# Strassen's seven block products in the up projection of a one-core decoder layer

## The chip, the cores and the metric

The kernel runs on one core of a Trainium2 chip. The metric is the device time of one execution in microseconds (us), the median of several. A core has TensorE (PE in the profile; its weight loads are PEld), VectorE (DVE), ScalarE (ACT), GpSimd (POOL) and SyncE (SP), which here issues every DMA. Each works through its own queue of instructions and waits on semaphores for the others.

## The reference

One decoder layer over 2048 tokens (and 16 meta tokens) of width 1024, all in float32. A first part mixes tokens (a state-space mixer, a retention mixer and an output projection) and normalises. What the change is about is the MLP behind it:

```python
h = layer_norm(DEEPNORM_ALPHA * h + mixed, ln1_g[l], ln1_b[l])
ff = jnp.square(jax.nn.relu(h @ w_up[l])) @ w_down[l]     # w_up 1024 x 4096, w_down 4096 x 1024
h = layer_norm(DEEPNORM_ALPHA * h + ff, ln2_g[l], ln2_b[l])
```

## The kernel before

**Blocks and phases.** The tokens are taken in two blocks of 1024 (`NB = 2`, b = 0 and 1). For each block, phase 1 makes the input projection and both mixers, phase 2 the output projection and first norm, and phase 3 the MLP. Phase 3 walks over the 4096 hidden units in eight groups (g) of four pages of 128 units (`G = 4`, f). A group has an up part (each page times 512 tokens at a time, twice) and a down part (eight tiles of 128 tokens, two halves of 512 output columns each, accumulated on VectorE into `acc`).

**Three products for one.** Every float32 operand is held as a rounded high part and a low part (value minus high part) in the type fp32r, and each product is made as high x high + high x low + low x high. So `mm3` (L265) issues three matmuls for each pair of 128 x 128 weights and 512 moving columns. A group is 8 x 8 x 3 = 192 matmuls up and 16 x 4 x 3 = 192 down.

**Weight pages.** `feed_init` (L123) lists all pages in the order in which they are used. `feed_raw` (L145) has SP load the raw 512-KB page into one of two buffers (`wraw`), as far as one page ahead; a load waits until the last reader of its buffer is done. `feed_one` (L154) splits a page: ScalarE copies the high part (L169), VectorE subtracts it for the low part (L171). At most eight pages live at once; `free` gives one back. `get` makes a page at once if it isn't there.

**Order.** The program order of each engine is the order in which the Python code emits instructions (`manual_schedule`). What is put between the matmuls is set by `tick` (L65): it runs callbacks that are due, one step of a background generator (`pump`), and one `feed`. In phase 3 there is a tick at half and at the end of every 24-matmul product of the up part (`marks=(3, 7)`), and one in each 12-matmul tile of the down part (`marks=(3,)`), ahead of that tile's addition. `rest_norm` (L469) is such a generator: in block 0 it normalises the eight token tiles of block 1, one in nine steps.

**Results of the up part.** A product sits in one of four PSUM banks of the pool `big`. ScalarE takes the relu (L1149) and its square as the high part (L1150), VectorE squares again (L1151) and subtracts (L1152). In the down part VectorE adds each PSUM tile to `acc` (L1179; in group 0 L1176).

Of the kernel before, what the change touches and what calls it, by code (L numbers as in the profile page):

```python
# [17 lines left out]
D = 1024  # L18
SEQ = 2048
NM = 16  # L20
NH = 6
# [11 lines left out]
KORDER = (2, 3, 4, 5, 6, 0, 1, 7)  # L33
ALPHA = 2.0 ** 0.25
# [9 lines left out]
class Builder:  # L44
    def __init__(self, tc, a, ctx):
# [7 lines left out]
        self.pgp = pool(name="pgp", bufs=8)  # L53
        self.ffp = pool(name="ffp", bufs=4)
        self.wrawp = pool(name="wrawp", bufs=2)
        self.bigp = pool(name="bigp", bufs=4, space=PSUM)
# [66 lines left out]
    def feed_init(self):  # L123
        a = self.a
        items = []
        for b in range(NB):
            slab = [[("s", b, h, p), a["wslab"][h, p], "w"] for h in range(NH) for p in range(4)]
            wo = [[("o", b, k), a["w_out"][k * 128:(k + 1) * 128, :], "w"] for k in KORDER]
            wu = [[("wu", b, i), a["wu"][i], "u"] for i in range(2)]
            items += slab[:4] + wu + slab[4:] + wo  # L130
            for g in range(NF // G):
                items += [[("u", b, g * G + f), a["wup"][g * G + f], "w"] for f in range(G)]
                items += [[("d", b, g * G + f), a["w_down"][(g * G + f) * 128:(g * G + f + 1) * 128, :], "w"]
                          for f in range(G)]
        self.items = items
        self.page = {}
        self.live = 0
        self.wu_ok = False
        self.pool_lo = False
        self.feed_every = 1  # L140
        self.ri = 0
        self.si = 0
        self.raws = {}

    def feed_raw(self):  # L145
        while self.ri < len(self.items) and self.ri < self.si + 2:
            key, src, kind = self.items[self.ri]
            if kind != "b":
                t = self.wrawp.tile([128, 1024], F32, tag="wraw", name="wraw")
                self.nc.sync.dma_start(out=t, in_=src)  # L150
                self.raws[self.ri] = t
            self.ri += 1

    def feed_one(self):  # L154
        if self.si >= len(self.items):
            return False
        key, src, kind = self.items[self.si]
        if (self.live >= 8 and kind != "u") or (kind == "u" and not self.wu_ok):
            return False
        self.feed_raw()  # L160
        if kind != "u":
            self.live += 1
        if kind != "b":
            t = self.raws.pop(self.si)
            if kind == "w":
                pg = self.pgp.tile([128, 2, 1024], F32R, tag="pg", name="pg")
            else:
                pg = self.ffp.tile([128, 2, 1024], F32R, tag="ff", name="wu")
            self.nc.scalar.copy(pg[:, 0, :], t)  # L169
            e = self.nc.gpsimd if self.pool_lo else self.nc.vector  # L170
            e.tensor_tensor(out=pg[:, 1, :], in0=t, in1=pg.bitcast(F32)[:, 0, :], op=ALU.subtract)  # L171
        else:
            pg = self.pgp.tile([128, 2, 1024], F32, tag="pg", name="pg")
            self.nc.sync.dma_start(out=pg, in_=src.partition_broadcast(128))
        self.page[key] = pg
        self.si += 1
        self.feed_raw()
# [12 lines left out]
    def free(self, key):  # L190
        del self.page[key]
        if key[0] != "wu":
            self.live -= 1
# [40 lines left out]

    def norm_v(self, t, gb, parts=1, st=None):
# [12 lines left out]
    def to_channels(self, t, hi, lo, tok, n=128):  # L248

        nc = self.nc  # L250
        for kk in range(2):
            ps = self.sm().rearrange("p (k t) -> p k t", k=4)
            for i in range(4):
                k = kk * 4 + i
                nc.tensor.transpose(ps[:, i, :n], t[:n, k * 128:(k + 1) * 128], self.ident[:n, :n])  # L255
# [9 lines left out]
    def mm3(self, ps, pairs, marks=(), pumps=(), first=True, last=True, done=None):  # L265
# [5 lines left out]
        for j, (lh, ll, rh, rl) in enumerate(pairs):  # L271
            for l, r in ((lh, rh), (lh, rl), (ll, rh)):
                nc.tensor.matmul(ps, l, r, start=(i == 0), stop=(i == n - 1))  # L273
# [9 lines left out]
    def build(self):  # L283
        nc, a = self.nc, self.a
        with self.tc.manual_schedule():
# [14 lines left out]
            self.y_d = [[dt(f"y{b}_{k}", [128, TB]) for k in range(8)] for b in range(NB)]  # L300
            self.um_d = dt("um", [NM, S5W])
# [5 lines left out]
            self.tab_d = [dt(f"tab{g}", [128, 2, 256]) for g in range(NG)]  # L307
            for b in range(NB):
                with ExitStack() as s:
                    self.p1 = s.enter_context(self.tc.tile_pool(name=f"p1_{b}", bufs=1))  # L310
                    self.phase1(b)
                    self.phase2_open(b)
                with ExitStack() as s:
                    self.accp = s.enter_context(self.tc.tile_pool(name=f"acc_{b}", bufs=1))
                    self.phase2(b)
                    self.phase3(b)


    def phase1(self, b):
# [29 lines left out]
        for h in range(NH):  # L349
            slab = [self.get(("s", b, h, p)) for p in range(4)]  # L350

            def part(k, i, c0, c1):
                return slab[k // 2][:, i, (k % 2) * 512 + c0:(k % 2) * 512 + c1]
# [115 lines left out]
    def rest_norm(self):  # L469
        nc = self.nc  # L470
        gb = self.gb_rest
        for t in range(NT, NB * NT):
            x = self.accp.tile([128, D], F32, tag="tmp", name="xr", bufs=2)
            nc.sync.dma_start(out=x, in_=self.a["x"][t * 128:(t + 1) * 128, :])
            for _ in range(3):
                yield
            self.norm_v(x, gb)
            for _ in range(4):
                yield
            nc.sync.dma_start(out=self.h_d[t], in_=x)  # L480
            for _ in range(2):
                yield
# [572 lines left out]
    def out_pairs(self, t, hf, k0, k1):  # L1055
        y, c = self.ys[t], slice(hf * 512, hf * 512 + 512)
        wo = lambda k: self.get(("o", self.b, k))
        return [(y[:, 0, k], y[:, 1, k], wo(k)[:, 0, c], wo(k)[:, 1, c]) for k in KORDER[k0:k1]]
# [218 lines left out]
```

## Time and profile before

| what | value |
|---|---|
| time, median of 3 runs | 2498.85 us (2496.75 to 2501.19) |
| the profiled execution | 2497.59 us, span 2495.8 us |
| granted TensorE clock, mean | 0.991 of full speed |
| PE, DVE, ACT, POOL busy in that span | 97%, 51%, 24%, 11% |
| DMA | 200.83 MB, mean 80 GB/s |

The span is the time from the first to the last instruction. Busy shares are means over a program whose phases differ; a busy PE is not PE at its peak, since matmuls are pipelined. Phase 3 takes most of the time: its groups follow each other at about 87 us.

### The profile page before, as it was taken

The numbers are of one execution on the slowest core, as the hardware profiler recorded it, in microseconds if no ns is written. First come the engines' busy times: TensorE is split into PE (matmuls) and PEld (weight loads), VectorE is DVE, ScalarE is ACT, GpSimd is POOL, SyncE is SP. The second block draws the span as 40 slices with busy tenths as digits, with TensorE's granted clock in tenths as the row PEclk, the third lists the DMA queues.
The fourth block names the chain that finished last, engine by engine and source line by source line (L and its number), as shares of the span: only waits on it lengthen the run. The fifth ranks groups of instructions, "written<-read, shape, count | busy, mean of one in ns | idle before, by whom it ended". The sixth has DMA issues, their size and how long they took to land. (4 is left out here: it accounts for less than half of the span.)

```text
span 2495.8 us, 30353 instructions
## 1 busy us (share of the span) xinstructions
PE 2410.0 (97%) x11932; PEld 2066.4 (83%) x11932; DVE 1285.2 (51%) x2770; ACT 602.8 (24%) x1151; POOL 265.2 (11%) x303
## 2 busy tenths in 40 slices
PE   6889999899999999999999999999999999999998
PEld 5778889778888888888889999988888888888886
DVE  6867757656455443334365455656634333333436
ACT  3323322322221122112132222222212212211211
POOL 2322322201000000000031011101000000000004
PEclk9999999999999999999999999999999999999999
DMA  5132253362132221102142422134212111110211
GB/s 198 65 101 86 86 125 101 91 196 68 59 102 86 72 71 60 48 28 68 51 144 90 97 90 78 62 108 158 83 36 68 51 34 51 59 51 26 68 34 68
DMA packets 100767, 200.83 MB, mean 80 GB/s; under 512 B 11360, under 2 KB 52096, under 8 KB 99984
## 3 DMA queue, kind: packets, MB, share of 16 engines
q1 hardware_dynamic: 100624, 198.88, 25.2%
q8 instruction: 94, 1.54, 0.3%
q14 instruction: 49, 0.40, 0.1%
HBM read 160.83 MB, written 39.06 MB: 80 GB/s over the span
## 5 line engine op out<-in xcount | busy, mean ns | idle before, releaser
L273 PE MATMUL big<-act,pg 128*128 128x512 f32 x3648 | 846.5, 391 | 0.0
L273 PEld LDWEIGHTS big<-act,pg 128*128 128x128 f32 x3648 | 681.1, 188 | 142.3 <-issue 2.4
L273 PE MATMUL big<-pg,ff 128*128 128x512 f32 x3072 | 700.8, 389 | 0.0
L273 PEld LDWEIGHTS big<-pg,ff 128*128 128x128 f32 x3072 | 576.1, 188 | 119.3
L273 PE MATMUL big<-pg,act 128*128 128x384 f32 x2304 | 458.7, 349 | 0.8 <-ACT act L256 0.5
L273 PEld LDWEIGHTS big<-pg,act 128*128 128x128 f32 x2304 | 404.3, 192 | 5.3 <-DVE act L257 1.4
L169 ACT CAST pg<-wraw 128x1024 fp32r<-128x1024 f32 x192 | 198.3, 1047 | 624.8 <-PE big L273 549.8
L1179 DVE TENSOR_TENSOR acc<-acc,big 128x512 f32<-128x512 f32 x224 | 153.1, 686 | 357.4 <-PE big L273 357.2
L1151 DVE TENSOR_TENSOR rs<-rs 128x512 f32<-128x512 f32 x128 | 88.5, 691 | 338.3 <-ACT rs L1149 338.2
L171 DVE TENSOR_TENSOR pg<-wraw,pg 128x1024 fp32r<-128x1024 f32 x175 | 211.4, 1222 | 64.7 <-ACT pg L169 58.1
L219 POOL TENSOR_TENSOR ln_rs<-ln_rs,mhalf 128x1 f32<-128x1 f32 (+1 forms) x49 | 61.4, 1253 | 1531.8 <-DVE ln_rs L218 1522.4
L273 PE MATMUL big<-pg,yt 128*128 128x512 f32 x768 | 182.5, 396 | 0.8 <-DVE yt L1008 0.7
L1149 ACT ACTIVATE rs<-big 128x512 f32<-128x512 f32 x128 | 76.6, 598 | 438.1 <-PE big L273 432.5
L273 PEld LDWEIGHTS big<-pg,yt 128*128 128x128 f32 x768 | 144.4, 190 | 32.7 <-DVE yt L1008 2.5
L1152 DVE TENSOR_TENSOR ff<-rs,ff 128x512 fp32r<-128x512 f32 x128 | 88.7, 693 | 14.0 <-DVE rs L1151 0.9
L519 DVE TENSOR_TENSOR t<-big,rope 128x256 f32<-128x256 f32 x96 | 40.5, 422 | 96.6 <-ACT v L512 96.2
L1150 ACT ACTIVATE ff<-rs 128x512 fp32r<-128x512 f32 x128 | 81.0, 633 | 4.1
L534 ACT COPY qkT<-sm 128x256 f32<-128x256 f32 x96 | 35.4, 369 | 156.4 <-PE sm L532 156.2
L550 DVE SCALAR_TENSOR_TENSOR R<-R,sm 128x128 f32<-128x128 f32 x96 | 27.3, 284 | 71.4 <-PE sm L549 71.3
L574 POOL TENSOR_TENSOR gn_sc<-gn_sc,mhalf 128x4 f32<-128x4 f32 x24 | 24.8, 1032 | 345.3 <-DVE gn_sc L572 325.2
L512 ACT ACTIVATE v<-big,cols 128x128 f32<-128x128 f32 x96 | 35.5, 369 | 100.4 <-PE big L273 100.4
L555 ACT COPY o<-sm 128x128 f32<-128x128 f32 x96 | 25.5, 266 | 139.3 <-DVE gn_st L553 134.2
(202 smaller groups left out, 1882.5 us busy)
## 6 DMA issues: line engine op xcount, KB each, us to landing
wraw<-in_wup_dram SPq DMA_DIRECT2D x64, 512.0 KB, 3.7
wraw<-in_w_down_dram SPq DMA_DIRECT2D x64, 512.0 KB, 3.7
wraw<-in_wslab_dram SPq DMA_DIRECT2D x48, 512.0 KB, 3.7
smat<-mat SPq DMA_DIRECT2D x32, 256.0 KB, 3.9
wraw<-in_w_out_dram SPq DMA_DIRECT2D x16, 512.0 KB, 3.8
acc<-h SPq DMA_DIRECT2D x16, 512.0 KB, 3.8
out_dram<-acc SPq DMA_DIRECT2D x14, 512.0 KB, 2.7
y<-yst SPq DMA_DIRECT2D x24, 256.0 KB, 3.3
```

The costliest lines, as they stand in the source:

```text
L169: self.nc.scalar.copy(pg[:, 0, :], t)
L171: e.tensor_tensor(out=pg[:, 1, :], in0=t, in1=pg.bitcast(F32)[:, 0, :], op=ALU.subtract)
L219: nc.gpsimd.tensor_tensor(out=rs[:n, 0:1], in0=rs[:n, 0:1], in1=self.mhalf[:n, 0:1], op=ALU.pow)
L273: nc.tensor.matmul(ps, l, r, start=(i == 0), stop=(i == n - 1))
L512: nc.scalar.activation(out=v2, in_=ps[:, 256:384], func=AF.Copy, scale=self.cols[:, h:h + 1])
L519: nc.vector.tensor_tensor(out=t1, in0=src, in1=c, op=ALU.mult)
L534: nc.scalar.copy(qkT, pt[:, 0:256])
L1149: nc.scalar.activation(out=tmp[:, 0], in_=ps, func=AF.Relu)
L1150: nc.scalar.activation(out=ff[f][:, 0, tk], in_=tmp[:, 0], func=AF.Square)
L1151: nc.vector.tensor_tensor(out=tmp[:, 1], in0=tmp[:, 0], in1=tmp[:, 0], op=ALU.mult)
L1152: nc.vector.tensor_tensor(out=ff[f][:, 1, tk], in0=tmp[:, 1], in1=ff[f].bitcast(F32)[:, 0, tk], op=ALU.subtract)
L1179: nc.vector.tensor_tensor(out=acc, in0=acc, in1=ps, op=ALU.add)
```

## The change

Groups from `CLASSIC[b]` on (2 in block 0, 1 in block 1; 13 of the 16 groups) make their up part with `up_seven`. A pair of pages (q) is seen as a 2 x 2 block matrix (two pages by two halves of the 1024 inputs), and the block of tokens as two halves by two halves. Strassen's algorithm in Winograd's form makes the four result blocks from seven block products in place of eight. A product p is 4 x 3 matmuls for each of the two pairs. Weight sums (`COMBO`) are made on VectorE as each page is fed. Sums of activation blocks are made once for each token block by `left_sums` (for each of four k, eight additions and four splits into high and low part on VectorE, in five steps; eight stores), during the last group of the old kind, and stored in DRAM; one of them is then loaded over a part of `h1T`, the other three are streamed back in every group by `ring_fill`. Results are put together by additions on VectorE from three accumulator banks (A, B, C) for each pair. The background generator `rest_norm` starts a group earlier and takes four steps a tile. Weight pages become units of 512 columns (two to an old page, 16 live), and phase 3 has a pool of 24 pieces of 128 x 512 (`q`, 2 KB in each partition) for hidden activations, sums, the ring and temporaries. The core of the diff:

```diff
+CLASSIC = (2, 1)
+PORDER = (6, 1, 5, 7, 2, 4, 3)
+COMBO = {1: ((None, 0, 0),), 2: ((None, 0, 1),), 3: ((None, 1, 1),),
+         4: ((None, 0, 1), (SUB, 1, 1), (ADD, 1, 0), (SUB, 0, 0)), 5: ((None, 1, 0), (SUB, 0, 0)),
+         6: ((None, 1, 1), (SUB, 1, 0), (ADD, 0, 0)), 7: ((None, 1, 1), (SUB, 1, 0))}
...
+        def pair(key, src1, src2):
+            n = len(self.srcs)
+            self.srcs += [src1, src2]
+            for p in PORDER:
+                self.jobs.append((key + (p,), COMBO[p], (n, n + 1)))
...
     def feed_raw(self):
+        while self.si < len(self.jobs) and self.ri < len(self.srcs) and self.ri < self.jobs[self.si][2][0] + 2:
+            t = self.wrawp.tile([128, 1024], F32, tag="wraw", name="wraw")
+            self.nc.sync.dma_start(out=t, in_=self.srcs[self.ri])
...
     def feed_one(self):
+        need = 0 if kind == "u" else 2 if kind == "w" else 1
+        if self.live + need > 16 or (kind == "u" and not self.wu_ok) or (need == 1 and self.qp is None):
             return False
...
+        elif kind == "w":
+            pg = [self.unit(), self.unit()]
+            for z in range(2):
+                nc.scalar.copy(pg[z][:, 0, :], raw[0][:, z * 512:z * 512 + 512])
+            for z in range(2):
+                e.tensor_tensor(out=pg[z][:, 1, :], in0=raw[0][:, z * 512:z * 512 + 512],
+                                in1=pg[z].bitcast(F32)[:, 0, :], op=ALU.subtract)
         else:
+            pg = self.unit()
+            src = [(op, raw[j][:, z * 512:z * 512 + 512]) for op, j, z in kind]
+            x = src[0][1]
+            if len(src) > 1:
+                t = self.q()
+                for op, y in src[1:]:
+                    nc.vector.tensor_tensor(out=t, in0=x, in1=y, op=op)
+                    x = t
+                self.qfree()
+            nc.scalar.copy(pg[:, 0, :], x)
+            nc.vector.tensor_tensor(out=pg[:, 1, :], in0=x, in1=pg.bitcast(F32)[:, 0, :], op=ALU.subtract)
...
+    def relu2(self, x):
+        nc.vector.scalar_tensor_tensor(out=x, in0=x, scalar=0.0, in1=x, op0=ALU.max, op1=ALU.mult)
+        hi = self.q(F32R)
+        nc.scalar.copy(hi, x)
+        lo = self.q(F32R)
+        nc.vector.tensor_tensor(out=lo, in0=x, in1=hi.bitcast(F32), op=ALU.subtract)
...
+    def left_sums(self, b):
...
+        def split(f, x, k):
+            hi = self.q(F32R)
+            S.copy(hi, f)
+            lo = self.q(F32R)
+            add(lo, f, hi.bitcast(F32), SUB)
+            for i, z in enumerate((hi, lo)):
+                nc.sync.dma_start(out=self.s_d[b][x][:, k, i], in_=z.bitcast(F32))
+            self.qfree(3)
+        for k in range(4):
+            x21, f1 = self.q(), self.q()
+            add(x21, hf[:, k, t2], lf[:, k, t2])
+            add(f1, hf[:, k + 4, t2], lf[:, k + 4, t2])
+            add(f1, f1, x21)
+            yield
...
+    def ring_fill(self, cap):
+        while self.stream and len(self.ring) < cap:
+            x, k = self.stream.popleft()
+            ts = [self.q(F32R) for _ in range(2)]
+            for i in range(2):
+                self.nc.sync.dma_start(out=ts[i].bitcast(F32), in_=self.s_d[self.b][x][:, k, i])
+            self.ring.append(ts)
...
+    def up_seven(self, b, g):
+        for p in PORDER:
+            bank = {1: "A", 2: "A", 6: "B", 7: "B", 4: "B", 5: "C", 3: "C"}[p]
+            first = p in (1, 6, 5)
...
+            w = [self.get(("U", b, g, q, p)) for q in range(NQ)]
+            for k in range(4):
+                if p in left:
+                    k0, tk = left[p]
+                    ah, al = h1[:, k0 + k, tk], l1[:, k0 + k, tk]
+                else:
+                    ah, al = self.ring.popleft()
+                for q in range(NQ):
+                    c = slice(k * 128, k * 128 + 128)
+                    self.mm3(acc[bank, q], [(w[q][:, 0, c], w[q][:, 1, c], ah, al)],
+                             first=first and k == 0, last=k == 3, more=not first)
+                if p not in left:
+                    self.qfree(2)
+                if self.stream:
+                    self.ring_fill(6 if self.stream[0][0] != 2 else 3 if p == 3 else 0)
+                if k == 1:
+                    self.tick()
+            for q in range(NQ):
+                self.free(("U", b, g, q, p))
+                ps, fa, fb = acc[bank, q], 2 * q, 2 * q + 1
+                if p == 6:
+                    s12[q] = self.q()
+                    S.copy(s12[q], ps)
+                elif p == 1:
+                    s21[q] = self.q()
+                    V.tensor_tensor(out=s12[q], in0=s12[q], in1=ps, op=ADD)
+                    S.copy(s21[q], ps)
+                elif p == 5:
+                    s22[q] = self.q()
+                    V.tensor_tensor(out=s22[q], in0=s21[q], in1=ps, op=ADD)
+                elif p == 2:
+                    x = self.q()
+                    S.copy(x, ps)
+                    ff[fa][0] = self.relu2(x)
+                else:
+                    x, f, h = {7: (s22, fb, 1), 4: (s21, fa, 1), 3: (s12, fb, 0)}[p]
+                    V.tensor_tensor(out=x[q], in0=x[q], in1=ps, op=ADD)
+                    ff[f][h] = self.relu2(x.pop(q))
+            self.tick()
...
+            to = list(range(NT)) if g < nc0 else [4, 0, 1, 2, 3, 5, 6, 7] if last else [4, 5, 6, 7, 0, 1, 2, 3]
...
+            if g == nc0 - 1:
+                self.drain_bg()
+                for i in range(2):
+                    nc.sync.dma_start(out=self.h1T[i].bitcast(F32)[:, 0:4, 512:1024], in_=self.s_d[b][1][:, :, i, :])
+                self.qfree(16)
+                self.ring_fill(6)
```

## Rows read from the trace of the kernel before

**Rows 1.** The page, part 1: busy us, share of the span, instructions.
```profile
PE 2410.0 (97%) x11932; PEld 2066.4 (83%) x11932; DVE 1285.2 (51%) x2770; ACT 602.8 (24%) x1151; POOL 265.2 (11%) x303
```

**Rows 2.** The chain that ended last: start us, us, what.
```profile
1637.35 2.09 PE big L273 x12
...
1802.24 677.34 PE big L273 x2988
```

**Rows 3.** Stretch of one group of phase 3: busy us by engine, clock, DMA.
```profile
1976.00:2063.00 87.00, 87.00 (x385) 72.05 (x384) 31.52 (x40) 17.49 (x25) 0.00 (x0) 1.00 0.15 48
```

**Rows 4.** Waits in 1802 to 2480: us in total, times, longest.
```profile
ACT pg L169 <- PE big L273: 274.9, 7, 39.3
...
DVE acc L1179 <- PE big L273: 190.9, 99, 2.0
...
ACT pg L169 <- DMA wraw<-in_w_down_dram: 7.3, 3, 4.8
```

**Rows 5.** Groups by shape: count, busy us, mean ns of one.
```profile
L1179 DVE TENSOR_TENSOR acc<-acc,big 128x512 f32<-128x512 f32 x224 | 153.1, 686 | 357.4 <-PE big L273 357.2
...
L256 ACT CAST act<-sm 128x512 fp32r<-128x512 f32 x64 | 34.3, 589 | 96.1 <-PE sm L255 96.1
```

**Rows 6.** Timeline of VectorE: start us, us, line.
```profile
695.34 0.69 DVE L1176 SCALAR_TENSOR_TENSOR acc<-acc,big 128x512 f32<-128x512 f32 x1 [2.03 <-PE big L273]
695.94 2.35 DVE L171 TENSOR_TENSOR pg<-wraw,pg 128x1024 fp32r<-128x1024 f32 x2
701.41 0.69 DVE L1151 TENSOR_TENSOR rs<-rs 128x512 f32<-128x512 f32 x1 [3.11 <-ACT rs L1149]
702.20 0.69 DVE L1152 TENSOR_TENSOR ff<-rs,ff 128x512 fp32r<-128x512 f32 x1
```

**Rows 7.** Timeline of ScalarE, and of VectorE behind it.
```profile
1995.44 0.60 ACT L1149 ACTIVATE rs<-big 128x512 f32<-128x512 f32 x1 [4.18 <-PE big L273]
1996.07 0.63 ACT L1150 ACTIVATE ff<-rs 128x512 fp32r<-128x512 f32 x1
1996.61 1.03 ACT L169 CAST pg<-wraw 128x1024 fp32r<-128x1024 f32 x1
...
1996.07 0.69 DVE L1151 TENSOR_TENSOR rs<-rs 128x512 f32<-128x512 f32 x1 [3.95 <-ACT rs L1149]
```

**Rows 8.** Timelines of VectorE, SP and ScalarE around one reload of `wraw`.
```profile
2057.52 2.36 DVE L171 TENSOR_TENSOR pg<-wraw,pg 128x1024 fp32r<-128x1024 f32 x2
...
2058.77 6.52 SPq L150 DMA_DIRECT2D wraw<-in_wup_dram  x3
...
2062.63 1.05 ACT L169 CAST pg<-wraw 128x1024 fp32r<-128x1024 f32 x1 [0.65 <-DMA wraw<-in_wup_dram]
```

**Rows 9.** All loads of `wraw` in 1802 to 2480, from issue.
```profile
DMA to landing us min/median/max: 3.4/3.7/5.9
```

**Rows 10.** Stretches around the last matmul, same columns as rows 3.
```profile
2484.00:2486.00 2.00, 1.00 (x5) 0.50 (x3) 1.24 (x2) 1.17 (x1) 2.00 (x1) 1.00 0.00 0
2486.00:2488.00 2.00, 0.00 (x0) 0.00 (x0) 1.97 (x3) 0.00 (x0) 0.77 (x2) 1.00 0.47 193
2488.00:2490.00 2.00, 0.00 (x0) 0.00 (x0) 1.86 (x4) 0.00 (x0) 2.00 (x2) 0.74 0.17 70
2490.00:2492.00 2.00, 0.00 (x0) 0.00 (x0) 2.00 (x4) 0.00 (x0) 0.74 (x1) 0.50 0.63 262
```

**Rows 11.** Timeline of PE near the start.
```profile
21.19 1.97 PE L255 MATMUL sm<-ident,x 128*128 128x128 f32 x8 [4.65 <-DVE x L245]
22.81 5.23 PE L273 MATMUL big<-pg,act 128*128 128x384 f32 x24
```

**Rows 12.** DMA issues: count, KB each, median us to landing.
```profile
gb<-in_ln_gb_dram SPq DMA_DIRECT2D x4, 1024.0 KB, 5.5
```

**Rows 13.** Timeline of VectorE: one tile of `rest_norm`, first and last instruction.
```profile
704.15 1.28 DVE L206 BATCH_NORM_STATS2 ln_st<-xr 128x6 f32<-128x512 f32 x2
...
707.49 1.28 DVE L245 SCALAR_TENSOR_TENSOR xr<-xr,ln_rs,gbrest 128x1024 f32<-128x1024 f32 x1 [0.43 <-POOL ln_rs L219]
```

More of the change, by code (lines that the diff above doesn't have):

```diff
@@ L145, in feed_raw @@
     def feed_raw(self):
[L146 to L151, printed above, removed]
+        while self.si < len(self.jobs) and self.ri < len(self.srcs) and self.ri < self.jobs[self.si][2][0] + 2:
+            t = self.wrawp.tile([128, 1024], F32, tag="wraw", name="wraw")
+            self.nc.sync.dma_start(out=t, in_=self.srcs[self.ri])
+            self.raws[self.ri] = t
@@ L159, in feed_one @@
             return False
         self.feed_raw()
[L161 to L171, printed above, removed]
-        else:
-            pg = self.pgp.tile([128, 2, 1024], F32, tag="pg", name="pg")
-            self.nc.sync.dma_start(out=pg, in_=src.partition_broadcast(128))
+        nc = self.nc
@@ new lines, in feed_one @@
+        raw = [self.raws[i] for i in ids]
+        e = nc.gpsimd if self.pool_lo else nc.vector
+        if kind == "u":
+            pg = self.ffp.tile([128, 2, 1024], F32R, tag="ff", name="wu")
+            nc.scalar.copy(pg[:, 0, :], raw[0])
+            e.tensor_tensor(out=pg[:, 1, :], in0=raw[0], in1=pg.bitcast(F32)[:, 0, :], op=ALU.subtract)
+        elif kind == "w":
[5 more added lines that the diff above has]
+                                in1=pg[z].bitcast(F32)[:, 0, :], op=ALU.subtract)
+        else:
+            pg = self.unit()
[9 more added lines that the diff above has]
+            nc.vector.tensor_tensor(out=pg[:, 1, :], in0=x, in1=pg.bitcast(F32)[:, 0, :], op=ALU.subtract)
@@ L263, in act_pair, with mm3 @@
         return hi, lo
-    def mm3(self, ps, pairs, marks=(), pumps=(), first=True, last=True, done=None):
+    def mm3(self, ps, pairs, marks=(), pumps=(), first=True, last=True, done=None, more=False):
         nc = self.nc
@@ L300, in build @@
             self.y_d = [[dt(f"y{b}_{k}", [128, TB]) for k in range(8)] for b in range(NB)]
+            self.s_d = [[dt(f"sum{b}_{x}", [128, 4, 2, 512]) for x in range(5)] for b in range(NB)]
             self.um_d = dt("um", [NM, S5W])
@@ new lines, in phase3 @@
+    def phase3(self, b):
+        nc, a = self.nc, self.a
+        ng = NF // G
+        nc0 = CLASSIC[b]
+        more = b + 1 < NB
+        self.b = b
+        self.stream = deque((x, k) for _ in range(nc0, ng) for x in (2, 3, 4) for k in range(4))
+        self.ring = deque()
+        for g in range(ng):
+            if g == 0 and more:
+                self.bg.append(self.rest_norm())
+            if g == nc0 - 1:
+                self.drain_bg()
+                self.q_open(b)
+                self.bg.append(self.left_sums(b))
+            last = g == ng - 1
+            ff = self.up_first(b, g) if g < nc0 else self.up_seven(b, g)
+            to = list(range(NT)) if g < nc0 else [4, 0, 1, 2, 3, 5, 6, 7] if last else [4, 5, 6, 7, 0, 1, 2, 3]
@@ new lines, in phase3 @@
+                for i in range(2):
+                    for hf in range(2):
+                        nc.sync.dma_start(out=gb2[i][hf],
+                                          in_=a["ln2_gb"][i, hf * 512:hf * 512 + 512].partition_broadcast(128))
+                if more:
+                    self.hT = self.act_pair()
+            for n, t in enumerate(to):
+                if last and more:
+                    x = [self.q(), self.q()]
+                    for hf in range(2):
+                        nc.sync.dma_start(out=x[hf], in_=self.h_d[(b + 1) * NT + t][:, hf * 512:hf * 512 + 512])
+                end = last and n == NT - 1
@@ L1179, in phase3 @@
                         nc.vector.tensor_tensor(out=acc, in0=acc, in1=ps, op=ALU.add)
-                    if last and t == NT - 1:
+                    if end:
                         if hf == 0:
```

257 lines of the change are left out of this document (180 added, 77 removed).

## The prediction, made before the change was run

> **What bounds the kernel now.** I read the page first, then the chain that ended last, then phase 3 by stretches and waits. TensorE is busy for 97% of the span, VectorE for 51% [rows 1]. That is a mean; the change sits in phase 3, and there the chain of block 1 is one piece: 2988 matmuls in 677.34 us with no gap [rows 2], so 0.2267 us a matmul. A group of 384 takes 87.05 us. In such a stretch VectorE works 31.5 us with 40 instructions, ScalarE 17.5 [rows 3]. The waits agree: ScalarE and VectorE wait for TensorE, not the reverse [rows 4]. So before, TensorE is the bound and VectorE has 55 us to spare in each group.
>
> Two rows matter later. Where a raw page is not there, the page copy at the head of ScalarE's queue holds up the queue, in one case for 4.8 us [rows 4]; nothing behind it runs. And VectorE's work is now spread one or two instructions at a time.
>
> **What the change removes.** Seven products for eight: 24 of the 192 up matmuls of a group, 24 x 0.2267 = 5.44 us, in 13 groups 70.7 us. Nothing else gets cheaper on TensorE.
>
> **What it adds on VectorE.** Counted from the code for a middle group: weight sums 2+0+1+1+0+3+0 = 7 for a pair, so 14; low parts of 14 units and of 8 half pages, 22; additions and `relu2` of the results 2+2+6+4+6+6 = 26; `acc` 16. Together 78 where 40 stood. One 128 x 512 instruction takes 0.69 us [rows 5]; the next starts 0.60 us after it if independent (695.34 to 695.94) and 0.80 if it reads its result (701.41 to 702.20) [rows 6]. ScalarE's copy of 512 takes 0.60 [rows 5], the next starts 0.54 after, and VectorE follows 0.03 after ScalarE's end [rows 7]. So 47 to 62 us of VectorE in 81.6 us of matmuls (360 x 0.2267): enough on the mean. What decides is where they stand in the queue.
>
> **The queue, worked through for a middle group.** Zero is its first matmul. A product takes 24 x 0.2267 = 5.44, so products 6, 1, 5, 7, 2, 4, 3 end at 5.4, 10.9, 16.3, 21.8, 27.2, 32.7 and 38.1. Each has two ticks, so two feeds. VectorE is in time up to product 7: the six remaining weight units of the second pair and the first down page are made by 20.9. Then, in program order:
> - Product 7, two blocks: add, square, (copy on ScalarE), low part. One block costs 0.80 + 0.72 + 0.63 + 0.60 = 2.75, because the low part waits for ScalarE and the next block waits behind it. 21.2 to 26.7.
> - Down pages 1 and 2, four low parts: to 29.2. Product 2 (two `relu2`): 29.3 to 33.5. Down page 3: to 34.7.
> - The tick in product 4 feeds the next group's unit 6, whose first sum reads the second source of a pair. `wraw` has two buffers; this source goes where down page 3 lay, so its load is issued when that page's low part ends, at 34.7. In the trace the same round goes from the end of a low part (2057.52 + 1.22) over an issue at 2058.77 to a copy at 2062.63: 3.9 us [rows 8]; all such loads land 3.4 to 5.9 us after issue, median 3.7 [rows 9]. No ring load is issued between, so SP isn't what delays it. VectorE stands from 34.7 to 38.6, with product 4's results queued behind, although they are there from 32.7.
> - Unit 6: two sums, copy, low part, to 41.4. Product 4: high parts at 43.5 and 46.2, low at 44.2 and 47.0.
>
> TensorE wants the first of these at 38.1 for down tile 4. It waits to 43.5, then to 46.2 for the second pair; the first down half tile ends at 47.9 in place of 40.8: 7.1 us lost.
>
> VectorE goes on with next units 1 and 5, product 3 (49.4 to 55.0), units 7 and 2, and only at 57.5 takes the first down sum out of PSUM. There are four banks, so the fifth half tile waits to 58.2 (would be 56.05): 2.1. Unit 4 (four instructions and a copy) holds the next: 1.4. Unit 6 of the second pair again reads a source loaded only after unit 3's low part: a second hole, 62.9 to 66.8, and the eighth half tile waits 2.5. From there VectorE catches up, and the next group starts clean. Together 13.1 us lost for 5.4 saved: **+7.7 us a group**.
>
> Bounds, by the same steps: loads at 3.4 and instructions at 0.63 (between 0.60 and 0.69) give 9.4 lost; loads at 5.0 give 16.5. So +3.9 to +11.0.
>
> The last groups have no next unit behind down page 3: in block 1 nothing is fed, 0.3 lost, so -5.1; in block 0 the next pages are phase 1's (source loaded earlier, two low parts), 1.5 lost, so -3.9.
>
> **Clock.** After the last matmul the granted clock stays 1.00 for a while, then reads 0.74 and 0.50 [rows 10], and after a pause of 4.65 us 24 matmuls of 384 columns took 5.23 us [rows 11] where 12 take 2.09 elsewhere [rows 2]: 1.05 us more. The first wait here, 5.4 us, is longer than that pause. I cost it at nothing, because the fifth half tile waits 2.1 us for VectorE anyway; without that cover 11 x 1.05 = 12 us. The Trainium skill (TensorE: Matmul & The Clock Gate, "HAM oscillation — how this bites in real kernels") says that pauses between bursts of matmuls throttle the array to half, every time anew. By that rule, added up in full, the sum would be 2602, by mine 2590; the tail's rows agree that the clock falls, and no row shows it in phase 3.
>
> **What else moves.** `left_sums` adds 48 VectorE instructions (at least 29 us) and 16 copies to the last old group of each block, most of it in the up part, with steps that wait on ScalarE. Four PSUM banks cover 3 x 5.44 = 16 us of lateness. Bounds 0 and 20 each; I take 7, nearer the cover, so 14 in all. The reload into `h1T` is 2 MB; 1 MB lands in 5.5 us [rows 12]; product 5 wants it 10.9 us into the next group, and the ring stands behind it. In block 0 the sums are done early; in block 1 they end six ticks before: 0 to 6, I take 3. `rest_norm` costs 4.6 us of VectorE a tile (704.15 to 708.8) [rows 13], now every four ticks, 10.9 us; group 0's slack covers it; uncovered, one tile's 4.6 once. Half pages: two copies and two low parts for one each, about 0.1 us a page, hidden since pages are made ahead; uncovered, 64 pages x 0.1 = 6. The ring adds 24 x 256 KB = 6 MB to a group's 4: the DMA share goes from 0.15 [rows 3] to about 0.4, SP issues 24 more. I cost it at nothing, hidden because the ring is six pairs deep; if it slows loads, that is the 5.0 above.
>
> **Sum**, against the profiled execution's own 2497.59 (span 2495.8, 1.3 below the median): 11 x 7.7 = 84.7, minus 9.0, plus 17: 2497.6 + 92.7 = **2590**. Own range 2530 to 2645.
>
> **Rivals.**
> - *TensorE stays the bound* (the other side): VectorE's results come in time, as 62 us of work fit in 82, and its waits before are all for TensorE [rows 4]. Then -70.7, and with 0 to 17 for the sums 2427 to 2444. It needs the mean loss under 5.44 us a group; against it stands that 26 us of queue follow product 7's end while TensorE has 16 us to the down part. 0.14. The Trainium skill (Perfetto Trace Analysis, "Identifying the Most-Contended Engine") would have it so: the engine with the highest occupancy sets the time, and that stays TensorE. The group's rows agree for before; no row shows VectorE at this load.
> - *Late, but without the holes*: the loads are there in time. The same steps with no load wait lose 4.2 (at 0.63) to 6.8 us a group: 2497.6 + 11 x (-1.2 to +1.4) - 9 + 17 = 2492 to 2521. For it: loads are seldom waited for now [rows 4]. Against: both buffers are held by one pair until its last unit. 0.17.
> - *Worse*: loads at 5.0 and over beside the ring, and both `left_sums` groups at 20: 2497.6 + 121 - 9 + 43 = 2653. 0.07.
>
> **Numbers.** The forecast has 0.62. A measurement here can tell about 0.2%, 5 us. Faster by more: 0.14 and 0.03 of the second rival; within: 0.03; slower: 0.80. The range 2480 to 2645 leaves out the first rival and the upper half of the last.
>
> **What would show it.** VectorE near 75% busy in products 7 to 3 with two stands of about 3.9 us for `wraw`, one in product 4, one in the first down tiles; TensorE waiting some 5 us for `relu2`'s high part at the start of each down part, then for PSUM at half tiles five to eight; groups 95 us apart. It is wrong if TensorE runs through the turn from up to down; if groups are 82 us apart, the first rival holds. If TensorE waits inside the products, for the ring or a weight unit, my view of SP is wrong.

## The result and the profile after

The changed kernel takes 2638.93 us (median; 2635.18 to 2641.7), the kernel before 2499.09 in runs beside it: a ratio of 1.0559, 95% interval 1.0541 to 1.0577. The forecast was 2590, range 2480 to 2645. The profiled execution took 2641.7 us, span 2639.9, mean granted clock 0.966. It answers to [rows 1] with this line of the page (engine, busy us, share, instructions):

```profile
PE 2409.3 (91%) x11620; PEld 2039.5 (77%) x11620; DVE 1603.4 (61%) x3445; ACT 668.2 (25%) x1427; POOL 265.7 (10%) x334
```

TensorE has 312 matmuls fewer, as 13 groups by 24 should give, and yet as many busy microseconds: some of its matmuls ran at a lower clock, as shown below. Both engines have room on the mean, 9% and 39% of the span. The loss is in waits, so the next view is the waits in block 1's seven-product groups, six middle ones and the last (us in total, times, longest), beside [rows 4]:

```profile
ACT pg L215 <- PE big L340: 141.6, 7, 23.0
...
DVE q L212 <- DMA wraw<-in_wup_dram: 40.8, 12, 4.2
PE big L340 <- ACT q L1263: 31.1, 6, 5.8
PE big L340 <- DVE acc L1424: 26.0, 18, 2.1
```

Before, only the slack engines waited, nearly always for TensorE. Now TensorE waits as well: once in each middle group, 5.2 us, for ScalarE's high part in `relu2` (L1263), and three times, 1.4 us each, for VectorE to empty a PSUM bank (L1424). VectorE stands twice in each, 3.4 us, for a raw source in `wraw` (L212). The chain of block 1, one unbroken piece in [rows 2], has no counterpart: followed back from its end, the profile's chain breaks off after 2 us and says nothing here.

One middle group of block 0, as [rows 3] (busy us by engine, granted clock, DMA share, GB/s): its up part and the wait behind it, the rest, and the whole.

```profile
1192.40:1230.50 38.10, 38.10 (x169) 31.36 (x167) 22.06 (x34) 12.97 (x23) 0.00 (x0) 1.00 0.41 136
1230.50:1288.20 57.70, 47.96 (x193) 37.85 (x193) 28.83 (x44) 7.75 (x13) 0.00 (x0) 0.94 0.28 93
1192.40:1288.20 95.80, 86.06 (x361) 69.22 (x360) 50.89 (x78) 20.72 (x36) 0.00 (x0) 0.96 0.33 110
```

VectorE has the 78 instructions that were counted, 50.9 us in 95.8. The up part runs without a gap. The down part in TensorE's timeline (start us, us, line, idle time before and what ended it):

```profile
1235.52 12.83 PE L340 MATMUL big<-pg,q 128*128 128x512 f32 x48 [4.86 <-ACT q L1263]
1250.26 3.02 PE L340 MATMUL big<-pg,q 128*128 128x512 f32 x12 [1.91 <-DVE acc L1424]
1254.35 5.74 PE L340 MATMUL big<-pg,q 128*128 128x512 f32 x24 [1.07 <-DVE acc L1424]
1261.99 26.38 PE L340 MATMUL big<-pg,q 128*128 128x512 f32 x108 [1.91 <-DVE acc L1424]
```

And VectorE's queue around its two stands:

```profile
1225.83 1.29 DVE L203 TENSOR_TENSOR pg<-wraw,pg 128x512 fp32r<-128x512 f32 x2
1230.65 0.69 DVE L212 TENSOR_TENSOR q<-wraw 128x512 f32<-128x512 f32 x1 [3.54 <-DMA wraw<-in_wup_dram]
...
1234.08 0.69 DVE L1261 SCALAR_TENSOR_TENSOR q<-q 128x512 f32<-128x512 f32 x1
...
1258.49 0.69 DVE L212 TENSOR_TENSOR q<-wraw 128x512 f32<-128x512 f32 x1 [3.00 <-DMA wraw<-in_wup_dram]
```

With the group's first matmul, 1192.4, as zero, this can be laid beside the forecast's queue:

| step | forecast | trace |
|---|---|---|
| down page 3's low part ends | 34.7 | 34.7 |
| first stand ends | 38.6 | 38.25 |
| TensorE starts the down part (wanted at 38.1) | 43.5 | 43.1 |
| lost up to the fourth half tile's end | 7.1 | 7.0 |
| lost before the fifth, sixth, eighth half tile | 2.1, 1.4, 2.5 | 1.9, 1.4, 2.2 |
| second stand ends | 66.8 | 66.1 |
| lost from there to the end | 0 | 1.7 |
| lost in all, against 5.4 saved | 13.1 | 14.2 |

Losses are starts in the timeline less 0.2267 us for each matmul between. The one line that the forecast lacks is the clock's: the last 108 matmuls took 26.2 us up to the next group and not 24.5. By stretches of the profile (PEclk is the figure before the DMA share):

```profile
1235.50:1238.50 3.00, 2.98 (x7) 2.00 (x8) 2.23 (x4) 0.90 (x2) 0.00 (x0) 0.50 0.00 0
1238.50:1248.20 9.70, 9.70 (x42) 7.71 (x42) 6.90 (x11) 2.64 (x6) 0.00 (x0) 0.98 0.00 0
1250.20:1260.10 9.90, 8.76 (x36) 6.61 (x36) 5.87 (x10) 1.24 (x3) 0.00 (x0) 1.00 0.41 132
1261.90:1266.00 4.10, 4.01 (x11) 3.15 (x12) 1.83 (x4) 0.00 (x0) 0.00 (x0) 0.60 0.67 208
```

After the 4.86 us wait the granted clock stands at the lower of its two levels (0.50, 1.2 of 2.4 GHz) for 3 us. That costs nothing more, for two reasons. Six slow matmuls, the first pair's, fill the time until the second pair's high part is there at 1238.2 (45.8 from zero); the forecast had TensorE wait for that until 46.2, and no such wait shows:

```profile
1237.60 0.62 ACT L1263 CAST q<-q 128x512 fp32r<-128x512 f32 x1 [2.14 <-DVE q L1261]
```

And the next half tile waits for VectorE anyway. After the waits of 1.91 and 1.07 us the clock reads 1.00; after the fourth wait, again 1.91 us, it reads 0.60 on the mean of 4 us, and this time nothing covers it. The group before has the same four waits and no second fall:

```profile
1141.42 13.71 PE L340 MATMUL big<-pg,q 128*128 128x512 f32 x48 [5.38 <-ACT q L1263]
1156.17 3.04 PE L340 MATMUL big<-pg,q 128*128 128x512 f32 x12 [1.04 <-DVE acc L1424]
1167.80 24.78 PE L340 MATMUL big<-pg,q 128*128 128x512 f32 x108 [1.81 <-DVE acc L1424]
```
```profile
1167.70:1171.80 4.10, 4.00 (x18) 3.31 (x19) 2.52 (x5) 0.00 (x0) 0.00 (x0) 1.00 0.65 208
```

The first fall is longer there, and the next wait shorter by as much: 13.71 and 1.04 us add up to what 12.83 and 1.91 do. So it is in all eleven middle groups. At the fourth wait seven of them lose some 1.7 us to the clock (waits of 1.87 to 2.12 us) and four lose nothing (1.80 to 2.57 us): 1.1 us a group on the mean. The length of that wait doesn't decide it; what does is not shown. The prediction weighed a rule of the Trainium skill (TensorE: Matmul & The Clock Gate, "HAM oscillation — how this bites in real kernels"), that pauses between bursts throttle the array every time anew. The trace agrees for the longest pause of each group; of the three shorter ones only the last does so, in seven groups of eleven, and only this one shows in the time.

**Where the 144.1 us between the two profiled spans are** (starts of groups in TensorE's timeline, before and after):

| stretch | before | after | difference | forecast |
|---|---|---|---|---|
| block 0 group 0, `rest_norm` | 88.8 | 100.5 | +11.7 | 0 |
| the two groups with `left_sums`, and the reload | 87.0, 88.9 | 102.0, 102.7 | +28.8 | +17 |
| 11 middle groups | 87.0 each | 95.7 each | +95.3 | +84.7 |
| last group, block 0 | 94.1 | 106.7 | +12.6 | -3.9 |
| last group, block 1 | 98.0 | 92.4 | -5.6 | -5.1 |
| everything else | | | +1.3 | 0 |

### The profile page after: what moved, and what is told of

It reads as the page before. It is cut to its first block, busy times and chain, and to the rows that moved or that the text cites. A ratio compares the mean times of both kernels' runs of the same rounds, so it can differ in the third digit from the quotient of the medians.

```text
span 2639.9 us, 31560 instructions
## 1 busy us (share of the span) xinstructions
PE 2409.3 (91%) x11620; PEld 2039.5 (77%) x11620; DVE 1603.4 (61%) x3445; ACT 668.2 (25%) x1427; POOL 265.7 (10%) x334
## 5 line engine op out<-in xcount | busy, mean ns | idle before, releaser
L340 PE MATMUL big<-pg,q 128*128 128x512 f32 x2880 | 714.9, 410 | 127.7 <-ACT q L1263 67.2
L340 PEld LDWEIGHTS big<-pg,q 128*128 128x128 f32 x2880 | 563.0, 198 | 276.1 <-ACT q L1263 79.4
L340 PE MATMUL big<-act,pg 128*128 128x512 f32 x1776 | 453.7, 394 | 0.0
L340 PEld LDWEIGHTS big<-act,pg 128*128 128x128 f32 x1776 | 330.0, 188 | 68.8 <-issue 2.4
L1424 DVE TENSOR_TENSOR acc<-acc,big 128x512 f32<-128x512 f32 x224 | 150.3, 684 | 237.8 <-PE big L340 237.8
L201 ACT CAST pg<-wraw 128x512 fp32r<-128x512 f32 x280 | 159.4, 620 | 130.8 <-DMA wraw<-in_w_down_dram 50.9
L203 DVE TENSOR_TENSOR pg<-wraw,pg 128x512 fp32r<-128x512 f32 x246 | 157.8, 687 | 46.2 <-ACT pg L201 45.8
L340 PE MATMUL sm<-act,pg 128*128 128x512 f32 x624 | 175.3, 389 | 0.0
L340 PEld LDWEIGHTS sm<-act,pg 128*128 128x128 f32 x624 | 117.2, 188 | 24.3
L1263 ACT CAST q<-q 128x512 fp32r<-128x512 f32 x120 | 74.4, 620 | 229.9 <-DVE q L1261 203.7
L340 PE MATMUL big<-q,pg 128*128 128x512 f32 x468 | 131.5, 390 | 0.0
L340 PE MATMUL sm<-q,pg 128*128 128x512 f32 x468 | 131.5, 389 | 0.0
L212 DVE TENSOR_TENSOR q<-wraw 128x512 f32<-128x512 f32 x104 | 71.4, 686 | 81.0 <-DMA wraw<-in_wup_dram 81.0
L215 ACT CAST pg<-wraw 128x512 fp32r<-128x512 f32 x78 | 48.2, 617 | 284.5 <-PE big L340 284.5
```

What stands on the lines that cost most here:

```text
L201: nc.scalar.copy(pg[z][:, 0, :], raw[0][:, z * 512:z * 512 + 512])
L203: e.tensor_tensor(out=pg[z][:, 1, :], in0=raw[0][:, z * 512:z * 512 + 512], in1=pg[z].bitcast(F32)[:, 0, :], op=ALU.subtract)
L212: nc.vector.tensor_tensor(out=t, in0=x, in1=y, op=op)
L215: nc.scalar.copy(pg[:, 0, :], x)
L1263: nc.scalar.copy(hi, x)
L1424: nc.vector.tensor_tensor(out=acc, in0=acc, in1=ps, op=ALU.add)
```

## Experiments

The theory after the result: in the middle groups it is the order in VectorE's queue, with next-group weight units ahead of results that TensorE waits for, made worse by two stands for raw sources; rivals are the ring's DMA traffic and plain lack of VectorE time. Three smaller losses have causes of their own. Ratios are to the kernel before, with 95% intervals.

**1. No stands.** All weight sums read the first source of their pair, which is there early.

```diff
-            src = [(op, raw[j][:, z * 512:z * 512 + 512]) for op, j, z in kind]
+            src = [(op, raw[0][:, z * 512:z * 512 + 512]) for op, j, z in kind]
```

> The weight sums read the first source of a pair wherever the changed kernel reads the second; the number of instructions and loads stays, the weights are not the right ones. Theory (order: VectorE's queue stands still for a raw source, with finished products queued behind it): the two stands of 3.9 us in each middle group vanish, a group goes from 95.7 to about 89 us, 11 groups, 2639 - 70 = 2570 us (2555 to 2585). Rival (volume: VectorE has 78 instructions where 40 stood, and their sum is what costs): unchanged, 2639 within 6.

Measured: 2555.45 us, 1.0228 (1.0213 to 1.0243), 83 us less than the change. A middle group takes 88.6 us; no wait for `wraw` is left in it, and its turn in TensorE's timeline reads:

```profile
1107.66 1.92 PE L340 MATMUL big<-pg,q 128*128 128x512 f32 x6 [1.72 <-ACT q L1263]
1110.41 10.10 PE L340 MATMUL big<-pg,q 128*128 128x512 f32 x42 [0.83 <-ACT q L1263]
1122.41 3.02 PE L340 MATMUL big<-pg,q 128*128 128x512 f32 x12 [1.90 <-DVE acc L1424]
1126.44 30.22 PE L340 MATMUL big<-pg,q 128*128 128x512 f32 x132 [1.01 <-DVE acc L1424]
```

So the stands, with what they entail, are worth 7.1 us of a group's 14.1 lost. The other 7 are lost without them: the queue alone is late.

**2. The queue's order alone.** Nothing is fed in products 4 and 3; in the down part every second tick feeds. The same instructions, later.

```diff
         for p in PORDER:
+            self.feed_every = 1000000 if p in (4, 3) else 1
...
+            self.feed_every = 2 if g >= nc0 else 1
...
+                self.feed_every = 1
```

> No weight unit is fed during products 4 and 3, and the next group's units are fed at every second tick of the down part instead. Same instructions, same loads, another order. Theory (order): products 4 and 3 are taken out right behind down page 3, TensorE passes the turn with under 1 us lost, a middle group takes 82 to 84 us where it took 95.7, so 11 x 12.7 = 140 us less, about 2500 us (2485 to 2520). Rival (volume): unchanged, 2639 within 6, the loss only moves.

Measured: 2482.36 us, 0.994 (0.9925 to 0.9954): 157 us less than the change, and under the kernel before. The time is a little under the range expected. A middle group takes 82.6 us, 1.0 over what its matmuls need, and no wait of VectorE for `wraw` is left. One such group, and the start of its down part:

```profile
1138.27:1220.70 82.43, 82.18 (x361) 67.41 (x360) 50.82 (x78) 20.65 (x37) 0.00 (x0) 1.00 0.39 128
```
```profile
1178.15 42.71 PE L340 MATMUL big<-pg,q 128*128 128x512 f32 x186 [0.25 <-ACT q L1263]
```

VectorE works 50.8 us with 78 instructions, as in the change (50.9 with 78); DMA moves the same bytes in less time. Lack of VectorE time is ruled out as the cause, and so is the traffic by itself: the order of the queue, stands included, is what cost 13.1 us a group. The last group of block 0 fell too, from 106.7 to 97.6 us.

**3. No streaming.** The ring's tiles are slices of `h1T`, and the streamed loads are left out.

```diff
-            ts = [self.q(F32R) for _ in range(2)]
-            for i in range(2):
-                self.nc.sync.dma_start(out=ts[i].bitcast(F32), in_=self.s_d[self.b][x][:, k, i])
-            self.ring.append(ts)
+            self.qlive += 2
+            self.ring.append([z[:, k, 0:512] for z in self.h1T])
```

> The streamed sums are not loaded: products 6, 7 and 3 read a block of the activations that lies in SBUF (left out: the right operand); left_sums still makes and stores them. Theory (order): the loads of raw sources land as before, unchanged, 2639 within 8. Rival (stream: 6 MB more a group slow the raw loads and hold up SP's queue): at least 20 us faster, under 2619.

Measured: 2622.09 us, 1.0493 (1.0477 to 1.0508). 17 us, between what the two theories asked for: a middle group takes 94.4 us, 1.3 less. The stream has a small share, which the forecast had put at nothing. Some 0.3 us of the 1.3 are falls of the clock at the fourth wait, five here for seven.

**4. `rest_norm` without its norm.** Loads and stores stay; VectorE's arithmetic (`norm_v`) is left out.

> rest_norm loads and stores its tiles and leaves out the arithmetic of the norm on VectorE. If the 11.7 us that group 0 of block 0 lost in the changed kernel come from these eight norms in VectorE's queue at four ticks a tile: about 2627 us (2624 to 2630). If they come from the half pages or from the loads in SP's queue: 2639 within 4.

Measured: 2619.56 us, 1.0477 (1.0459 to 1.0496). Block 0's first group is back at 88.9 us, which is 11.7 less. The time fell by 19 us, more than was expected; the other 8 lie in no one place, and these runs lie 13 us apart. That the loss needs the norms is shown; how they cost 11.7 us is taken up in 8, 10, 11 and 12.

**5. Experiment 2, and the last group of block 0 loads its next-block tiles one tile ahead** and feeds at every tick. Why, show SP's queue and TensorE in the change:

```profile
1317.52 13.40 SPq L175 DMA_DIRECT2D wraw<-in_wslab_dram  x4
1331.81 7.03 SPq L175 DMA_DIRECT2D wraw<-in_wu_dram  x2
1338.89 1.85 SPq L1405 DMA_DIRECT2D q<-in_ln_gb_dram  x4
1340.78 16.56 SPq L1413 DMA_DIRECT2D q<-h  x8
```
```profile
1347.71 1.97 PE L322 MATMUL sm<-ident,q 128*128 128x128 f32 x8 [14.37 <-DMA q<-h]
```

Raw loads of phase 1's pages wait in SP's queue for VectorE to release `wraw`, and the tile loads stand behind them.

> e2_feed_later, and in the last group of block 0 the tiles of block 1 are loaded one tile ahead, with a feed at every tick there. Theory: in that group SP's queue stands behind raw pages that wait for VectorE's low parts, and the tiles' loads behind them; the group goes from 97.6 to about 90 us, 2474 us (2470 to 2479). Rival (what is lost there is the clock or VectorE): 2482 within 3.

Measured: 2481.75 us, 0.993 (0.9918 to 0.9943). The group falls from 97.6 to 90.2 us as forecast, but block 1's phases 1 and 2 rise from 475.6 to 479.8: most of the gain is given back, and the time can't be told from that of experiment 2, as the rival had it. In the next run, which keeps this edit, the first matmuls of phase 1 wait for the last tile's low part:

```profile
1310.83 7.08 PE L341 MATMUL big<-act,pg 128*128 128x512 f32 x23 [2.17 <-DVE act L325]
```

**6. Experiment 5, and half of `left_sums`' additions on GpSimd**, with no weight unit fed in the up part of that group.

```diff
+        def head(k):
+            ts = [self.q() for _ in range(3)]
+            for o, kk, t in zip(ts, (k, k + 4, k), (t2, t2, t1)):
+                nc.gpsimd.tensor_tensor(out=o, in0=hf[:, kk, t], in1=lf[:, kk, t], op=ADD)
+            return ts
...
+            nc.gpsimd.tensor_tensor(out=f4, in0=hf[:, k + 4, t1], in1=lf[:, k + 4, t1], op=ADD)
...
+            self.hold = g == nc0 - 1
```

`head` runs a step ahead; while `hold` is set, `feed_one` takes no unit of 512 columns. In the down part of that group, too, only every second tick feeds now. What each of these is worth by itself was not measured.

> e5_load_ahead, and left_sums makes four of its eight additions for each k on GpSimd, with VectorE work put between a split's copy and its low part; no weight sums are fed in the up part of that group. Theory (VectorE's queue is late in these two groups, by 14 us each): 10 us less in each, about 2454 us (2446 to 2464). Rival (GpSimd slows VectorE as much as it relieves it): 2474 within 5.

Measured: 2467.86 us, 0.9873 (0.9859 to 0.9886). This lies between what the two theories asked for. The two groups take 93.4 and 94.8 us (101.6 and 103.3 in 5). A new wait follows the first of them:

```profile
798.49 1.81 PE L341 MATMUL sm<-q,pg 128*128 128x512 f32 x3 [5.00 <-DMA q<-sum]
```

**7. Experiment 6 with a third old group in block 0**, `rest_norm` at eight ticks a tile over two of them.

> e6_sums_on_gpsimd with three groups of the old kind in block 0, rest_norm at eight ticks a tile over two of them. Theory: the 10 us lost to rest_norm come back, one seven-product group (4.5 us) is given up: 5 us less than e6, about 2449. Rival (rest_norm costs by its sum and not by its pace): 4 us more than e6.

Measured: 2475.3 us, 0.9896 (0.9881 to 0.9911), 7.4 more than 6. The groups did as expected (90.4 and 87.0 us: at that pace the norms cost little), but block 1's phases 1 and 2 took 489.0 us in place of 479.7. What this run changes there is still open.

**8. Experiment 6 with part of the norm on ScalarE and GpSimd.**

> e6_sums_on_gpsimd, and rest_norm at four ticks a tile, with the scaling on ScalarE and the last addition on GpSimd: VectorE has 3.1 us a tile instead of 4.6. Theory: 4 to 10 us less than e6, about 2447. Rival (the wait is for the tile's load, not for VectorE): within 3 of e6.

Measured: 2489.28 us, 0.9958 (0.9946 to 0.997): 21 us worse than 6, the group at 109.1 us. With fewer VectorE microseconds a tile it got longer, so VectorE's time alone is not the price. The run adds work on ScalarE and GpSimd, for which VectorE and the tile then wait; it doesn't tell these apart.

**9. Experiment 6 with the ring ahead of the reload.**

```diff
+                self.qfree(16)
+                self.ring_fill(6)
                 for i in range(2):
                     nc.sync.dma_start(out=self.h1T[i].bitcast(F32)[:, 0:4, 512:1024], in_=self.s_d[b][1][:, :, i, :])
-                self.qfree(16)
-                self.ring_fill(6)
```

> The version with the sums on GpSimd, with one order changed: at the end of the last old group SP issues the ring's first six pairs ahead of the 2-MB reload into h1T, not behind it. Theory: the waits of 5.0 us (block 0) and 5.8 us (block 1) for the ring at the head of the first seven-product group come from the reload's 2 MB ahead of the ring on SP's queue; product 5, which reads the reload, comes 10.9 us later and does not wait. Then these two groups fall from 84.2 and 83.9 us to about 82.3 each if little is left, and the time from 2467.9 to 2460 (2456 to 2466), since the waits stand at the start of groups and nothing else covers them. Rival: the ring waits for the stores of the sums themselves, which end late; then the waits stay, within 1 us, and the time stays at 2468 within 3 us. Second rival: the wait only moves to product 5, which then waits for the reload: the same time.

Measured: 2456.83 us, 0.9835 (0.982 to 0.9849), 11 less than 6. The first old-to-new turn has no wait any more:

```profile
792.10 0.84 PE L341 MATMUL sm<-q,pg 128*128 128x512 f32 x3
```

**10. Experiment 9, `rest_norm`'s next load right behind the present norm** and ahead of its store.

> The version with the ring first, and rest_norm with the load of its next tile issued right behind the norm of the present one, so four ticks ahead of its use and not two, and ahead of the present tile's store. VectorE's instructions are the same. Theory: block 0's first group is long because VectorE stands for the loads of the tiles (3.43 and 2.25 us in the down part of the version with the sums on GpSimd) in front of the sums of the down part, for which TensorE then waits 4.7 and 1.9 us. Then that group falls from 99.3 us to about 92 (90 to 94), and the time lies 7 us (4 to 10) under that of the version with the ring first. Rival: it is the 4.7 us of VectorE that each tile takes, whatever the loads do; then the group stays within 2 us of 99.

Measured: 2464.73 us, 0.987 (0.9854 to 0.9887): 8 us worse, the group at 110.6 us. My theory falls; the waits of that stretch say why. In the change:

```profile
ACT rs L1243 <- DMA h<-xr: 16.2, 2, 9.7
```

and here:

```profile
ACT rs L1250 <- DMA h<-xr: 40.2, 4, 12.1
...
PE big L341 <- ACT rs L1250: 10.4, 1, 10.4
```

The temporary of an up result (`rs`) and a tile of `rest_norm` (`xr`) take turns in the same two buffers (`tmp`). A relu that comes to the tile's buffer waits on ScalarE for the tile's store, and VectorE's squares behind it; here TensorE, too, waits once for such a relu. Holding a tile longer makes more of that. The kernel before has no such row.

**11. Experiment 9, one buffer of the two for `xr` alone, one for `rs`.**

```diff
-            x = self.stp.tile([128, D], F32, tag="tmp", name="xr", bufs=2)
+            x = self.stp.tile([128, D], F32, tag="tmp0", name="xr", bufs=1)
...
-                tmp = self.stp.tile([128, 2, 512], F32, tag="tmp", name="rs", bufs=2)
+                tmp = self.stp.tile([128, 2, 512], F32, tag="tmp1", name="rs", bufs=1)
```

> The version with the ring first, with one more edit: rest_norm's tile and the temporaries of block 0's first group (rs) no longer take turns in the same two 4-KB buffers of the tag tmp; each has one of the two for itself. No instruction is added or left out. Theory, from the version with the early load: after a relu that takes the buffer that held a tile, ScalarE waits for that tile's store (22.5 us in three waits in the version with the ring first, 40.2 us in four with the early load, none before the change, when a tile was held for fewer of the results), and VectorE's squares and sums wait behind it. Then ScalarE's waits for the store are gone and the group falls from 99.4 us to about 92 (90 to 95); what is left is VectorE's wait for the tile's load, which now cannot be issued before the store has landed. The time falls from 2456.8 to 2450 (2446 to 2453). Rival: the 4.7 us of VectorE of each tile are the cause, or the load alone; then the group stays at 98 or more, and the time within 3 us of 2457.

Measured: 2464.34 us, 0.9861 (0.9848 to 0.9874), the group at 106.6 us: 7 us worse, against the theory. Phase 2's loads, which had the same tag, take the two buffers in turn here. The waits for the store are gone, as said; others have come in their place (up to 708 us, most of the group):

```profile
DVE ln_st L252 <- DMA xr<-in_x_dram: 23.9, 6, 6.0
ACT rs L1244 <- DVE ff L1247: 21.5, 4, 10.7
```

With one buffer a load can't start before the store has landed, so VectorE waits for the load, and a relu waits for VectorE to be through with the one before.

**12. Experiment 11 with the norm three ticks behind its load, one ahead of its store.**

> The version before with the norm three ticks behind its load and one tick ahead of its store (two and two so far). If the rest of the loss is VectorE's wait for the load, which has one tick (2.7 us) more here, the group falls by another 2 us to about 90 (88.5 to 92) and the time to 2448 (2444 to 2452). If what is left is the room that the norms take in VectorE's queue, the group stays where the run with own buffers has it, within 1 us.

Measured: 2455.17 us, 0.9824 (0.9811 to 0.9838). The group falls by 9.7 to 97.0 us, as the theory has it in kind, but it started higher than was assumed and ends above the 90. The next one, where the eighth tile's end now lies, rises from 87.0 to 91.2; the time can't be told from that of 9. A third buffer was not tried.

## Why the prediction was right, and where it was off

**The range held in part by luck.** The time lies 49 us over the forecast and 6 under the upper end of the range. Between the profiled executions 144.1 us came where 92.7 were forecast: 11 of the 51 missed are in the middle groups, 41 in the terms beside them, each of which is taken up below. The room at the top of the range came mostly from slow raw loads in the middle groups (5.0 us), and these did not come: the median load of block 1's groups landed in 3.6 us, and a stand was 3.4 us on the mean, forecast 3.9.

**The middle groups: right, by the mechanism forecast.** The queue worked through by hand agrees with the trace within 0.7 us at each place of the first table up to the second stand, but for TensorE's second short wait, whose place a slow stretch of the clock took. Both stands are there; experiment 1 gives their worth, experiment 2 shows that order and not load is the cause. Two terms of the sum were mis-sized at nothing: the clock, 1.7 us in seven groups of eleven and 1.1 on the mean, since the fifth half tile's wait hides one fall and nothing hides the other, and the ring, some 1 us (experiment 3). A middle group loses 14.1 us, forecast 13.1.

**The rival that TensorE stays the bound** failed for this order, but experiment 2 meets it in the middle groups: 82.6 us where 81.6 is the least. The Trainium skill (Perfetto Trace Analysis, "Identifying the Most-Contended Engine") takes the engine of highest occupancy for the bottleneck. That names TensorE here, with PE at 91% of the span, its weight loads at 77% and DVE at 61%, but not the remedy: moving VectorE's instructions, none of TensorE's, took 157 us away. *Late, but without the holes* failed too, since both stands are there; without them (experiment 1) a group loses 7.0 us, just over the 4.2 to 6.8 of that rival.

**The last group of block 0: the step failed.** "The next pages are phase 1's (source loaded earlier, two low parts), 1.5 lost" looked at VectorE alone. Those pages' raw loads stood in SP's queue ahead of the loads of the next block's tiles, and TensorE waited 14.4 us for one of these: +12.6 for -3.9. This is a queue that a moved step passes, and I had not followed it. Experiment 2, which feeds later, took 9.1 us out of the group, and experiment 5 by loading earlier another 7.4.

**`rest_norm`: "group 0's slack covers it" failed.** VectorE has the time, and ScalarE too (71 and 25 of 100 us busy). Experiment 4 loads, holds and stores the same tiles in the same two buffers without the norms and takes 88.9 us, so neither the transfers nor the shared buffers cost anything by themselves. With the norms the waits point to the two buffers that tiles and temporaries share, at a tile every 10.9 us: 8, 10, 11 and 12 give 97.0 to 110.6 us with the same or less VectorE work. Which single step of the round costs what stays open, since each edit moved the wait elsewhere.

**`left_sums`: the term was mis-sized.** Forecast 14 and a reload of 3, measured 28.8, and none of it for the reload: in the change TensorE runs into the first group of seven products without a gap. The four PSUM banks do cover the up part; the loss comes behind it, in block 0:

```profile
761.35 13.24 PE L340 MATMUL big<-pg,q 128*128 128x512 f32 x51 [8.48 <-ACT q L1263]
777.48 31.82 PE L340 MATMUL big<-pg,q 128*128 128x512 f32 x132 [2.90 <-DVE acc L1424]
```

These two waits are 11.4 of the 15.0 us; the matmuls behind them took the other 3.6, at a granted clock of 0.95 on the mean of the group. Taking 16 additions off VectorE, holding the weight units back and feeding later (experiment 6) gave 8 us a group. The ring ahead of the reload gave another 6 and 5, most of it the wait that experiment 6 had brought up.

What is left in experiment 9, over the 70.7 us that the matmuls would save: 28 us, of which block 0's first group has 10.6, eleven middle groups 1.1 each, phases 1 and 2 of block 1 3.3, and the last group of block 0 2.4.

## What to carry to other kernels

Where an engine works in order, ask of each instruction that is fed in early who stands behind it: work for the next stage belongs behind results for which the bound engine waits now, and the mean load says nothing about it. Follow each queue and each shared buffer that a step passes, SP's and a pool's turns too: a tile that is held across a store, or a load that waits for its buffer, holds up whatever comes next in the same turn. Before a wait is removed, look for what takes its place: in experiments 5, 6, 11 and 12 something did.

## What the runs showed of the hardware that was not expected

GpSimd's additions slow VectorE's down. Groups by shape in the group with `left_sums` (count, busy us, mean ns), in the change, where VectorE does all of them:

```profile
L1280 DVE TENSOR_TENSOR q<-q 128x512 f32<-128x512 f32 x16 | 11.1, 692 | 0.6
```

and in experiment 6, where GpSimd does 16:

```profile
L1281 DVE TENSOR_TENSOR q<-q 128x512 f32<-128x512 f32 x16 | 14.5, 928 | 0.0
```

That is a mean: beside a GpSimd addition such an instruction takes up to 1.78 us, alone 0.68. The start of the group shows both kinds of VectorE instruction beside GpSimd:

```profile
708.01 1.27 DVE L1447 SCALAR_TENSOR_TENSOR acc<-acc,big 128x512 f32<-128x512 f32 x2
709.21 5.90 DVE L204 TENSOR_TENSOR pg<-wraw,pg 128x512 fp32r<-128x512 f32 x4
```
```profile
708.17 2.99 POOL L1294 TENSOR_TENSOR q<-act 128x512 f32<-128x512 f32 x2 [1.17 <-DVE xr L312]
711.12 1.74 POOL L1313 TENSOR_TENSOR q<-act 128x512 f32<-128x512 f32 x1
712.83 5.13 POOL L1294 TENSOR_TENSOR q<-act 128x512 f32<-128x512 f32 x3
```

Four instructions with both inputs in SBUF take 5.90 us, where four such took 2.49 in the change; two with one input in PSUM take 1.27 us, 0.68 each as in the change. The Trainium skill (SBUF — State Buffer, "Who interferes with whom") says that a VectorE instruction with two SBUF inputs shares a read port with a GpSimd instruction that reads SBUF, and one with a single SBUF input doesn't; both halves agree with these rows, the second on two instructions only. VectorE's busy time in that group rose, from 68 us to 74, with 12 instructions fewer, and the group was still 8 us shorter.
